# Weight loads as tasks of the planner, and tasks that look for a free buffer before they take one, in a one-core conformer and S5 decoder layer

## The chip, the core and the metric

The kernel runs on one core of a Trainium2 chip. The metric is the device time of one execution in microseconds (us). Three runs of the kernel before took 1961.82 us in the median (1961.4 to 1967.51).

## What is computed

One decoder layer is applied to 2048 new tokens of one sequence and to 8 single tokens of other sequences (`sample`). The width is 1024. The core of the reference:

```
h = rmsnorm(x, g_pre);  proj = h @ w_in            # 1024 -> 6144 columns
c_a, c_b, c_z, s_x, s_z, g_c, g_s = split(proj)    # 1024 x3, 512 x2, 1024 x2
u   = c_a * sigmoid(c_b)
v   = silu(layernorm(depthwise_conv31(u))) * silu(c_z);   y_c = v @ w_pc
ys  = gelu(ssm(s_x))                               # 32 groups x 64 complex states, scan over time
ys  = ys * sigmoid(ys @ w_glu + b_glu) * silu(s_z);       y_s = ys @ w_ps
m   = sigmoid(g_c) * y_c + sigmoid(g_s) * y_s
x   = x + rmsnorm(m @ w_out, g_post)
e   = rmsnorm(p @ w_ple, g_ple)
y   = x + e * sigmoid(x @ w_pg + b_pg)
```

The last rows of `u` and the last SSM state are outputs too.

## The kernel before

Channels lie on the partitions and tokens on the free dimension. The tokens are worked in two halves: h = 0 has 1032 of them (1024 and the 8 samples), in blocks of 344 columns, and h = 1 has 1024, in blocks of 512. In the two matrices at a half's end (`w_out`, `w_pg`) the first half goes by two parts of 516 columns, each in blocks of 258.

**Matmuls.** Weights and activations are split into a high and a low part, and each 128x128 tile of weights takes three matmuls: high by high, high by low, low by high (L289 to L291; the helper `stage_pair`, L307 to L309, does two chunks together). The low part of an activation is made on DVE or POOL after the high part was cast on ACT: `hh`/`hl` for the half's input, `mh`/`ml` for later ones.

**Weights.** The weights come in 194 chunks of 512 KB in a fixed list, `order`. A chunk is loaded into one of two `raw` buffers (`w_dma`), then split by `w_split`: ACT casts two `whi` tiles (L252), POOL subtracts to make two `wlo` tiles. There are four `whi` and four `wlo` tiles, so two chunks. `take`, which every matrix stage calls first, calls `w_ahead(i, ahead)`, and that splits the chunks up to i + ahead and issues loads up to i + 2 + ahead.

**The DMA queue.** Nearly every transfer is issued by SP, in program order (`dma`, L153). If a transfer waits for its buffer or for its data, the ones behind it wait too.

**Background work.** Everything besides the weight matmuls is written as generators, called tasks: the setting up of the SSM tables (`ssm_setup`), the SSM of a quarter of the groups (`ssm_batch`), the convolution, norms, gates. `Background` holds the tasks with priorities and keeps a clock for each engine from costs per instruction. A task yields an engine and the time from which it can go on. After each matmul block `pump` runs those tasks whose time has come, lowest priority number first. The order in which the tasks emit their instructions becomes the program order of every engine, and no engine leaves its program order. A change of one task's planned time can therefore move instructions on all engines.

**Buffers.** Large tiles come from 38 units (`Units`); `alloc` takes the next free one in the plan, and `room(k)` makes a task yield in steps of 0.5 us of planned time until k units are free.

**The places that matter below:**
- The SSM set-up. DVE builds a table of powers by seven doubling steps for each of two sets (`ph`), 12 small instructions a step, tiles of 8 up to 512 columns. Then it makes `gt`, which PE transposes (L610), and ACT copies the result into `we` (L613). The first convolution tile begins meanwhile: DVE sets its buffer's edge and starts `acc`, and ACT and POOL do a part of the 31 taps (`cq` on ACT, L882; the add to `ca` on POOL).
- The `re` sums: DVE or POOL adds squares (`rt`, squared on ACT) for a norm that is needed much later.
- The end of a half. DVE rescales the eight `o` tiles by the norm `oacc`, adds the residual `xr`, and ACT and DVE split them into `mh` and `ml` for `w_pg`. For each of eight channel tiles and each part, `y_task` loads `e`, makes `sgp` and stores it to `out_yT`.
- The boundary between halves. `next_h_task` loads eight tiles `xn`, scales them on DVE and splits them into `hh` and `hl`, which the first matmuls of h = 1 read.

## Time and profile before

| what | value |
|---|---|
| median of three runs | 1961.82 us (1961.4 to 1967.51) |
| the profiled execution | 1960.78 us |
| its span | 1959.0 us |
| mean granted clock of TensorE | 0.991 |
| PE busy | 1915.9 us (98%) |
| DVE busy | 1438.4 us (73%) |
| ACT busy | 769.3 us (39%) |
| POOL busy | 784.2 us (40%) |
| DMA queue 1, share of 16 engines | 37.0% |

The span is the time from the first to the last instruction of the profiled execution; the device time has 1.78 us around it. PE is the bound: it is idle for some 43 us in the span, part of it at the start and at the end. The rest of the idle time lies in a dozen places, the longest 14.06 us.

### The profile page before, as it was taken

The numbers are of one execution on the slowest core, as the hardware profiler recorded it, in microseconds if no ns is written. First come the engines' busy times: TensorE is split into PE (matmuls) and PEld (weight loads), VectorE is DVE, ScalarE is ACT, GpSimd is POOL, SyncE is SP. The second block draws the span as 40 slices with busy tenths as digits, with TensorE's granted clock in tenths as the row PEclk, the third lists the DMA queues.
The fourth block names the chain that finished last, engine by engine and source line by source line (L and its number), as shares of the span: only waits on it lengthen the run. The fifth ranks groups of instructions, "written<-read, shape, count | busy, mean of one in ns | idle before, by whom it ended". The sixth has DMA issues, their size and how long they took to land.

```text
span 1959.0 us, 27432 instructions
## 1 busy us (share of the span) xinstructions
PE 1915.9 (98%) x10772; PEld 1723.5 (88%) x10772; DVE 1438.4 (73%) x1703; ACT 769.3 (39%) x1301; POOL 784.2 (40%) x573
## 2 busy tenths in 40 slices
PE   8897999999999999999999999999999999999998
PEld 7897999999999999999997888888788888888876
DVE  6889997899899876446674579888499843341786
ACT  7424211228311364255533223455731353223542
POOL 1437523315422233234452222786743223224554
PEclk9898999999999999999999999999999999999999
DMA  8461334542122215334564563222112311432455
GB/s 316 152 209 56 106 133 142 181 141 71 57 89 80 99 43 194 120 95 144 193 207 162 183 204 119 65 65 97 66 43 76 99 65 44 161 108 86 140 193 172
DMA packets 103290, 243.63 MB, mean 124 GB/s; under 512 B 11752, under 2 KB 41576, under 8 KB 103144
## 3 DMA queue, kind: packets, MB, share of 16 engines
q1 hardware_dynamic: 102840, 241.68, 37.0%
q8 instruction: 84, 1.38, 0.3%
q14 instruction: 46, 0.38, 0.1%
q10 hardware_dynamic: 320, 0.20, 0.0%
HBM read 188.17 MB, written 54.62 MB: 124 GB/s over the span
## 4 chain that ended last, share of the span: by engine, by line
PE 84%; DVE 4%; issue 3%; POOL 2%; ACT 2%; DMA 1%; SPq 0%; ACTq 0%; POOLq 0%; DVEq 0%
PE bank L289 27%; PE bank L291 26%; PE bank L290 26%; PE bank L775 2%; POOL ca L332 1%; PE bank L778 1%; PE bank L720 1%; DVE sgp L332 1%; POOL wlo L332 1%; DVE o L183 1%; DMA raw<-in_w 1%; DVE spar L183 0%; DVE o L332 0%; PE bank L620 0%; DMA xn<-in_xT 0%
## 5 line engine op out<-in xcount | busy, mean ns | idle before, releaser
L332 POOL TENSOR_TENSOR wlo<-raw,whi 128x512 fp32r<-128x512 f32 x386 | 565.7, 1484 | 1072.2 <-ACT whi L252 1056.8
L289 PE MATMUL bank<-hh,whi 128*128 128x344 f32 (+1 forms) x1888 | 666.1, 353 | 0.9 <-ACT whi L252 0.9
L290 PE MATMUL bank<-hl,whi 128*128 128x344 f32 (+1 forms) x1888 | 661.4, 350 | 5.3 <-DVE hl L332 5.3
L291 PE MATMUL bank<-hh,wlo 128*128 128x344 f32 (+1 forms) x1888 | 659.8, 349 | 1.5 <-POOL wlo L332 1.5
L183 DVE SCALAR_TENSOR_TENSOR acc<-u,prm,acc 128x1024 f32<-128x1024 f32 x412 | 530.5, 1288 | 11.2
L289 PEld LDWEIGHTS bank<-hh,whi 128*128 128x128 f32 x1888 | 356.6, 189 | 37.5 <-ACT whi L252 1.5
L290 PEld LDWEIGHTS bank<-hl,whi 128*128 128x128 f32 x1888 | 357.1, 189 | 36.8 <-DVE hl L332 5.6
L291 PEld LDWEIGHTS bank<-hh,wlo 128*128 128x128 f32 x1888 | 357.4, 189 | 34.7 <-POOL wlo L332 2.5
L252 ACT CAST whi<-raw 128x512 fp32r<-128x512 f32 x388 | 223.9, 619 | 144.0 <-PE bank L290 68.7
L289 PE MATMUL bank<-mh,whi 128*128 128x258 f32 (+1 forms) x768 | 247.0, 322 | 2.2 <-ACT mh L339 1.7
L291 PE MATMUL bank<-mh,wlo 128*128 128x258 f32 (+1 forms) x768 | 246.6, 321 | 1.7 <-POOL wlo L332 1.6
L290 PE MATMUL bank<-ml,whi 128*128 128x258 f32 (+1 forms) x768 | 246.5, 321 | 0.4 <-DVE ml L332 0.3
L291 PEld LDWEIGHTS bank<-mh,wlo 128*128 128x128 f32 x768 | 145.6, 190 | 14.3 <-POOL wlo L332 3.0
L289 PEld LDWEIGHTS bank<-mh,whi 128*128 128x128 f32 x768 | 145.4, 189 | 14.2 <-ACT mh L339 1.9
L290 PEld LDWEIGHTS bank<-ml,whi 128*128 128x128 f32 x768 | 145.5, 189 | 12.5 <-DVE ml L332 1.0
L332 POOL TENSOR_TENSOR ca<-ca,cq 128x512 f32<-128x512 f32 x104 | 132.3, 1300 | 38.9 <-ACT cq L882 35.6
L290 PE MATMUL bank<-vl,whi 128*128 128x344 f32 (+1 forms) x320 | 111.9, 350 | 0.7 <-DVE vl L332 0.7
L289 PE MATMUL bank<-vh,whi 128*128 128x344 f32 (+1 forms) x320 | 112.0, 350 | 0.0
L291 PE MATMUL bank<-vh,wlo 128*128 128x344 f32 (+1 forms) x320 | 111.9, 350 | 0.0
L882 ACT ACTIVATE cq<-u,prm 128x512 f32<-128x512 f32 x104 | 73.4, 722 | 55.1 <-POOL ca L332 46.0
L332 DVE TENSOR_TENSOR oacc<-oacc,sq 128x258 f32<-128x258 f32 (+1 forms) x42 | 29.7, 721 | 70.2 <-ACT sq L1389 69.9
L177 DVE TENSOR_TENSOR gcl<-bank,gcl 128x344 f32<-128x344 f32 (+1 forms) x40 | 23.5, 587 | 65.4 <-PE bank L291 65.3
(213 smaller groups left out, 2452.0 us busy)
## 6 DMA issues: line engine op xcount, KB each, us to landing
raw<-in_w SPq DMA_DIRECT2D x194, 512.0 KB
cq<-cq SPq DMA_DIRECT2D x12, 512.0 KB
e<-e SPq DMA_DIRECT2D x8, 516.0 KB
rt<-e SPq DMA_DIRECT2D x8, 516.0 KB
gc<-gc SPq DMA_DIRECT2D x8, 516.0 KB
m<-gs SPq DMA_DIRECT2D x8, 516.0 KB
gcl<-gc SPq DMA_DIRECT2D x8, 516.0 KB
m2l<-m SPq DMA_DIRECT2D x8, 516.0 KB
```

The costliest lines, as they stand in the source:

```text
L177: V.tensor_tensor(out=out, in0=a, in1=b, op=op)
L183: V.scalar_tensor_tensor(out=out, in0=a, scalar=s, in1=b, op0=op0, op1=op1)
L252: S.copy(out=hi, in_=t[:, c])
L289: T.matmul(o, hi[:, w], rh[:, c0:c0 + n], start=kt == 0, stop=False)
L290: T.matmul(o, hi[:, w], rl[:, c0:c0 + n], start=False, stop=False)
L291: T.matmul(o, lo[:, w], rh[:, c0:c0 + n], start=False, stop=kt == k - 1)
L332: (V if e == "V" else GP).tensor_tensor(out=out, in0=a, in1=b, op=op)
L720: T.matmul(pvs[rr][half_[i], jj], we[:, g * P + rr * 64:g * P + rr * 64 + 64], U[:, g, 8:8 + ne], start=True, stop=True)
L775: T.matmul(pvs[i][:, jj], TW[:, :, 2 * j + i], U[:, 2 * j + i, o0:136], start=True, stop=False)
L778: T.matmul(pvs[i][:, jj], cq[half_[i], x * 512 + j * P:x * 512 + (j + 1) * P], X[half_[i], x, j, o0:136], start=False, stop=x == 1)
L882: S.activation(out=q[:, h], in_=u[:, k + x * 512:k + x * 512 + 512], func=AF.Identity, scale=w(k))
```

## The change

`w_ahead` no longer issues the loads that are ahead. For each it adds a task, `w_load_task(i)`, with a priority below all others' numbers, so it goes first; in the plan it waits until 0.8 us after the `raw` buffer of that chunk is free, and then issues the load. A split whose chunk has not been loaded still issues the load itself (`w_load`). Besides this, seven places of four tasks now yield until one or two units are free before they take one. Which instructions there are hardly changes: the matmuls are the same, POOL and ACT have a few more convolution taps and DVE fewer.

```diff
-        wstate = {"dma": 0, "split": 0, "use": 0, "raw": [0.0, 0.0]}
+        wstate = {"dma": 0, "asked": 0, "split": 0, "use": 0, "raw": [0.0, 0.0]}
...
+        def w_load(i):
+
+            while wstate["dma"] <= i:
+                w_dma(wstate["dma"])
+                wstate["dma"] += 1
+
+        def w_load_task(i):
+
+            yield None, wstate["raw"][i % 2] + 0.8
+            w_load(i)
+
         def w_ahead(i, ahead=1):
 
             while wstate["split"] < min(i + 1 + ahead, len(order)):
-                while wstate["dma"] <= wstate["split"]:
-                    w_dma(wstate["dma"])
-                    wstate["dma"] += 1
+                w_load(wstate["split"])
                 w_split(wstate["split"], "G" if wstate["split"] else "V")
                 wstate["split"] += 1
-            while wstate["dma"] < min(i + 3 + ahead, len(order)):
-                w_dma(wstate["dma"])
-                wstate["dma"] += 1
+            while wstate["asked"] < min(i + 3 + ahead, len(order)):
+                if wstate["asked"] >= wstate["dma"]:
+                    bg.add(w_load_task(wstate["asked"]), -5 + 1e-4 * wstate["asked"])
+                wstate["asked"] += 1
...
                 r1 = use("V", 6 * cV(512), r1)
+                yield from room(1)
                 we = alloc(name="we")
...
                 free(gt)
+                yield from room(1)
                 yield "V", r3
                 kdu = alloc(name="kd")
...
                 free(kdu, we)
+                yield from room(1)
                 cq = alloc(name="cq")
...
             r = max(r1, rp)
+            yield from room(2)
             tmp, tm2 = alloc(name="stmp"), alloc(name="stmq")
...
             def gelu_task(b):
+                yield from room(1)
                 yield "S", ready[b]
+                yield from room(1)
                 zs[b] = alloc(name="z")
...
             def ysn_task(b):
+                yield from room(2)
                 yield "S", ready[b]
+                yield from room(2)
                 ysn[b] = hilo("yn")
```

What moves is seen at three places.

**DVE in the SSM set-up**, where the first convolution tile begins (`u`, `usm`, `tails`, `acc`) among the steps of the doubling (`ph`, `spar`). Before:

```order
L177 TENSOR_TENSOR ph_1651<-ph_1649 128x8x2
L177 TENSOR_TENSOR ph_1651<-ph_1650 128x8x2
L177 TENSOR_TENSOR ph_1649<-ph_1651 128x8x2
L177 TENSOR_TENSOR ph_1651<-ph_1649,ph_1650 128x8x2
L177 TENSOR_TENSOR ph_1651<-ph_1650,ph_1649 128x8x2
L177 TENSOR_TENSOR ph_1650<-ph_1651 128x8x2
L828 MEMSET u_1457 128x30
L829 COPY usm<-u_1457 128x8
L832 COPY tails<-u_1457 128x30
L180 TENSOR_SCALAR acc<-u_1457,prm 128x1024
```

And now:

```order
L177 TENSOR_TENSOR ph_1305<-ph_1304,ph_1303 128x512
L177 TENSOR_TENSOR ph_1304<-ph_1305 128x8x64
L842 MEMSET u_1429 128x30
L843 COPY usm<-u_1429 128x8
L846 COPY tails<-u_1429 128x30
L180 TENSOR_SCALAR acc<-u_1429,prm 128x1024
L585 COPY ph_1721<-spar_725 128x8
L585 COPY ph_1722<-spar_725 128x8
L177 TENSOR_TENSOR spar_725<-ph_1721 128x8
```

The convolution's start stood behind the first two steps of the second set; it now stands ahead of the whole second set. On PE the first transposes of `gt` stand 48 matmuls later than before.

**SP at the boundary of the halves**: the loads of `xn`, of weights (`raw`) and the stores of the first half's outputs. Before, with the fourth `xn` first:

```order
L153 DMA xn_10370<-in_xT 128x1024
L153 DMA raw<-in_w 128x1024
L153 DMA e_10414<-e_89 128x516
L153 DMA out_yT<-sgp_10233 128x516
L153 DMA raw<-in_w 128x1024
L153 DMA xn_10460<-in_xT 128x1024
L153 DMA xn_10467<-in_xT 128x1024
L153 DMA xn_10474<-in_xT 128x1024
L153 DMA xn_10481<-in_xT 128x1024
L153 DMA out_yT<-sgp_10302 128x516
L153 DMA out_yT<-sgp_10378 128x516
L153 DMA raw<-in_w 128x1024 x2
```

And now, with the fifth `xn` first:

```order
L153 DMA xn_10316<-in_xT 128x1024
L153 DMA e_10355<-e_89 128x516
L153 DMA out_yT<-sgp_10245 128x516
L153 DMA raw<-in_w 128x1024
L153 DMA e_10424<-e_89 128x516
L153 DMA xn_10457<-in_xT 128x1024
L153 DMA out_yT<-sgp_10321 128x516
L153 DMA raw<-in_w 128x1024
L153 DMA xn_10477<-in_xT 128x1024
L153 DMA raw<-in_w 128x1024
L153 DMA xn_10486<-in_xT 128x1024
L153 DMA out_yT<-sgp_10390 128x516
```

The last four `xn` stood together behind the load of chunk 103; now the fifth stands ahead of the load of chunk 101, the sixth and seventh ahead of those of 102 and 103, and only the eighth behind 103.

**DVE and SP at the end of the first half**, in its second part. DVE before, up to the last `ml`, with the multiplications of `e` and `sgp` between:

```order
L183 SCALAR_TENSOR_TENSOR o_8114<-o_8114,prm,oacc_8116 128x516
L183 SCALAR_TENSOR_TENSOR o_8115<-o_8115,prm,oacc_8116 128x516
L183 SCALAR_TENSOR_TENSOR e_9606<-e_9606,prm,re_8669 128x516
L332 TENSOR_TENSOR sgp_9570<-sgp_9570,e_9606 128x516
L332 TENSOR_TENSOR sgp_9570<-sgp_9570,o_8112 128x516
L183 SCALAR_TENSOR_TENSOR e_9677<-e_9677,prm,re_8669 128x516
L332 TENSOR_TENSOR sgp_9641<-sgp_9641,e_9677 128x516
L332 TENSOR_TENSOR sgp_9641<-sgp_9641,o_8113 128x516
L332 TENSOR_TENSOR o_8114<-o_8114,xr_9713 128x516
L332 TENSOR_TENSOR o_8115<-o_8115,xr_9717 128x516
L332 TENSOR_TENSOR ml_7908<-o_8114,mh_7907 128x516
L332 TENSOR_TENSOR ml_8007<-o_8115,mh_8006 128x516
```

And now:

```order
L183 SCALAR_TENSOR_TENSOR o_8141<-o_8141,prm,oacc_8143 128x516
L183 SCALAR_TENSOR_TENSOR o_8142<-o_8142,prm,oacc_8143 128x516
L342 TENSOR_TENSOR sgp_9419<-sgp_9419,e_9453 128x516
L342 TENSOR_TENSOR sgp_9419<-sgp_9419,o_8137 128x516
L342 TENSOR_TENSOR o_8141<-o_8141,xr_9616 128x516
L342 TENSOR_TENSOR o_8142<-o_8142,xr_9646 128x516
L183 SCALAR_TENSOR_TENSOR e_9526<-e_9526,prm,re_8672 128x516
L342 TENSOR_TENSOR ml_7935<-o_8141,mh_7934 128x516
L342 TENSOR_TENSOR ml_8034<-o_8142,mh_8033 128x516
```

The last `ml` was the 45th instruction from the norm's first on; it is now the 33rd. On SP the load of chunk 93 stood behind one store of that stretch; it now stands behind three:

```order
L153 DMA raw<-in_w 128x1024
L153 DMA e_9765<-e_89 128x516
L153 DMA out_yT<-sgp_9492 128x516
L153 DMA out_yT<-sgp_9574 128x516
L153 DMA out_yT<-sgp_9654 128x516
L153 DMA raw<-in_w 128x1024
```

The last of these stores waits for the 41st DVE instruction from the norm's first on. The same two shifts are found at the end of the second half.

## Rows read from the trace of the kernel before

**Rows 1.** The page: busy times, and the chain that ended last by engine.

```profile
PE 1915.9 (98%) x10772; PEld 1723.5 (88%) x10772; DVE 1438.4 (73%) x1703; ACT 769.3 (39%) x1301; POOL 784.2 (40%) x573
...
PE 84%; DVE 4%; issue 3%; POOL 2%; ACT 2%; DMA 1%; SPq 0%; ACTq 0%; POOLq 0%; DVEq 0%
```

**Rows 2.** Waits of SP's queue: us in total, times, longest.

```profile
SPq L153 <- POOL wlo L332: 1218.7, 173, 20.0
...
SPq L153 <- DVE sgp L332: 61.7, 19, 21.5
```

**Rows 3.** Timeline of DVE: start, us, operation, idle before and its releaser.

```profile
104.14 1.23 DVE L332 TENSOR_TENSOR re<-re,rt 128x1032 f32<-128x1032 f32 x1 [4.85 <-ACT rt L985]
```

**Rows 4.** Timeline of ACT, about 107 us.

```profile
106.85 1.16 ACT L252 CAST whi<-raw 128x512 fp32r<-128x512 f32 x2
```

**Rows 5.** Stretches: length, PE, PEld, DVE, ACT, POOL busy, clock, DMA.

```profile
145.10:147.00 1.90, 1.90 (x14) 1.90 (x14) 1.69 (x15) 0.00 (x0) 0.00 (x0) 1.00 0.86 303
152.70:164.00 11.30, 11.30 (x73) 11.30 (x72) 11.09 (x14) 5.61 (x10) 11.03 (x9) 1.00 0.23 66
...
173.60:186.80 13.20, 8.57 (x55) 8.29 (x53) 12.99 (x13) 4.65 (x7) 13.00 (x10) 0.91 0.14 40
187.90:192.90 5.00, 0.00 (x0) 0.00 (x0) 4.79 (x14) 0.00 (x0) 0.00 (x0) 0.50 0.14 52
```

**Rows 6.** Timelines of DVE, PE and POOL around the first transposes.

```profile
195.44 0.69 DVE L177 TENSOR_TENSOR gt<-gw 128x512 f32<-128x512 f32 x1
...
196.23 0.66 PE L610 MATMUL bank<-ident,gt 128*128 128x128 f32 x2 [14.06 <-issue]
...
198.64 1.28 POOL L332 TENSOR_TENSOR ca<-ca,cq 128x512 f32<-128x512 f32 x1 [12.04 <-ACT cq L882]
```

**Rows 7.** Timelines of PE, ACT and SP's queue at the first half's end.

```profile
989.09 0.39 PE L289 MATMUL bank<-mh,whi 128*128 128x258 f32 x1 [1.67 <-ACT mh L339]
989.82 0.58 PE L290 MATMUL bank<-ml,whi 128*128 128x258 f32 x1 [0.35 <-DVE ml L332]
...
988.41 0.62 ACT L339 CAST mh<-o 128x516 fp32r<-128x516 f32 x1 [7.96 <-DVE o L332]
...
980.92 0.33 SPq L153 DMA_DIRECT2D raw<-in_w  x1
```

**Rows 8.** Stretches, as in group 5: the first half's end and the boundary.

```profile
952.00:990.30 38.30, 36.19 (x294) 35.37 (x293) 37.87 (x41) 15.01 (x31) 18.46 (x12) 0.99 0.63 197
...
980.00:1000.00 20.00, 17.98 (x133) 17.37 (x133) 17.59 (x19) 5.82 (x12) 10.20 (x7) 0.91 0.55 180
...
1040.00:1060.00 20.00, 18.08 (x71) 13.96 (x69) 9.56 (x9) 4.73 (x6) 0.00 (x0) 0.91 0.42 144
```

**Rows 9.** Timelines of SP's queue, DVE and PE at the boundary of the halves.

```profile
1039.84 2.55 SPq L153 DMA_DIRECT2D xn<-in_xT  x4
...
1046.49 1.28 DVE L183 SCALAR_TENSOR_TENSOR xn<-xn,prm,rb 128x1024 f32<-128x1024 f32 x1 [5.99 <-DMA xn<-in_xT]
...
1048.91 0.50 PE L307 MATMUL bank<-hh,whi 128*128 128x512 f32 x1 [1.16 <-ACT hh L339]
1050.17 0.49 PE L308 MATMUL bank<-hl,whi 128*128 128x512 f32 x1 [0.76 <-DVE hl L332]
...
1060.77 0.50 PE L308 MATMUL bank<-hl,whi 128*128 128x512 f32 x1 [0.43 <-DVE hl L332]
```

**Rows 10.** Second half's end: PE and ACT timelines, and a piece of the chain.

```profile
1901.07 0.50 PE L289 MATMUL bank<-mh,whi 128*128 128x512 f32 x1 [0.51 <-ACT whi L252]
1902.92 0.50 PE L291 MATMUL bank<-mh,wlo 128*128 128x512 f32 x1 [1.13 <-POOL wlo L332]
1915.13 0.51 PE L291 MATMUL bank<-mh,wlo 128*128 128x512 f32 x1 [0.51 <-POOL wlo L332]
...
1911.32 1.22 ACT L339 CAST mh<-o 128x512 fp32r<-128x512 f32 x2 [8.17 <-DVE o L332]
...
1904.59 3.57 DMA raw<-in_w
```

## The prediction

> **What bounds the kernel now.** I read the page first. PE is busy 1915.9 of 1959.0 us and carries 84% of the chain that ended last [rows 1]. The matmuls stay the same, so the change can only move what PE waits for. That is 43 us in all, and a gain can't be larger than that and the clock lost behind it.
>
> The next view is the waits of SP's queue [rows 2]. 173 waits for `wlo` add up to 1218.7 us: most of the time the queue's head is a weight load whose `raw` buffer is still in use. This is what the change is about. But a waiting head costs time only where something behind it is late for PE, and PE's own waits, read from the timelines, tell where that is:
>
> - the SSM set-up, 14.06 us before the first transposes of `gt` [rows 6]
> - the first half's end, 1.67 and 0.35 us for `mh` and `ml` [rows 7]
> - the boundary, 1.16, 0.76 and 0.43 us for `hh` and `hl`, which come from `xn` [rows 9]
> - the second half's end, 0.51, 1.13 and 0.51 us for split weights [rows 10]
>
> The remaining waits lie where the order does not change, or are shorter. I go through these four places with the new order.
>
> **The set-up.** Before: DVE stands 4.85 us until an `rt` square lets it go on at 104.14 [rows 3]. The stretches then show the doubling steps at two prices [rows 5]. The step of 16 columns took 1.90 us with POOL idle, that of 64 columns 11.30 with POOL busy, that of 256 columns 13.20 with POOL busy, and that of 512 columns only 5.00 when POOL had stopped. So beside POOL's adds a small DVE instruction takes 0.8 us in place of 0.1. POOL stopped because ACT, in program order, stands at its `we` copy and sends no `cq`: POOL was idle for 12.04 us up to 198.64 [rows 6], so the adds end at 186.6.
>
> Now three things differ.
>
> 1. The `rt` square stands on ACT behind a `whi` cast that ends at 108.0 [rows 4]. With about 1.1 for the square DVE goes on at 109.1, 5.0 later.
> 2. The convolution starts ahead of the second set, not behind two of its steps. Before, those steps ended at 147.0. Now it starts at 147.0 + 5.0 - 3.8 = 148.2 and ends near 149.5. The step of 8 columns follows to 151.4. POOL's adds begin near 152.4 as before (ACT is held by PE there).
> 3. ACT has 21 `cq` ahead of its `we` copy instead of 19, so the adds end at 186.6 + 2 x 1.28 = 189.2.
>
> The steps of 16, 32 and 64 columns fall under the adds: 3 x 11.3, and with three evictions of `u` 1.5, to 186.8. The step of 128 is half free, 4.0 (between 1.90 and 11.30), to 190.8. The step of 256 is free, 3.4 (between 1.90 and 5.00), to 194.2, and that of 512 ends at 199.2. Small ones and two more evictions take 2.8, half a `gt` 2.0: 204.0. Before it was 195.44 + 0.69 = 196.1 [rows 6], so `gt` comes 7.9 later. PE meanwhile does the 48 matmuls that now stand ahead of the transposes, 73 in 11.3 us [rows 5], so 7.4. Term: **+0.5**. PE's wait stays near 14 us and moves. Bounds: -6, if the steps of 16 and 32 columns under the adds cost nearer 8 than 11.3; above, the second rival.
>
> A rule of the Trainium skill speaks against this place. The page "SBUF — State Buffer", section "SBUF: two separate sides", says that DVE instructions with two SBUF inputs and GpSimd instructions that read SBUF take turns on a shared port pair, each holding it for its whole length. The prices of [rows 5] agree. By that rule alone the 24 instructions moved under the adds would come on top in full, which is the second rival's time; the rows add that the adds run out.
>
> **The first half's end.** 41 DVE instructions took 37.87 us there [rows 8], 0.92 each, and ACT stood 7.96 us for the last `o` [rows 7]. The last `ml` moves from the 45th to the 33rd instruction after the norm, so it is done 11 us sooner. That removes 1.67 + 0.35 and the clock behind it. The granted clock of 980 to 1000 is 0.91 [rows 8], a stretch at 1.2 GHz worth 0.09 x 20 = 1.8. Together -3.8. What is late next is the load of chunk 93. It was issued at 980.92 [rows 7], and now stands behind a store that needs the 41st DVE instruction. The 45th ended at 990.3, so the 41st at 986.6. With 3.57 to land [rows 10] the chunk is there at 990.3. Its split, before, came just behind the `mh` casts at about 990.3 and would be wanted 3.8 sooner: late by up to 3.8, by 0 if the chunk in PE's hands covers it. I take 1.5. Term: **-2.3**.
>
> **The boundary.** SP issued the last four `xn` together at 1039.84, and DVE stood 5.99 us for the first of them until 1046.49 [rows 9]. Now the fifth, sixth and seventh stand ahead of the loads of chunks 101 to 103, so they are issued from about 1028 on. Only the eighth is issued near 1040, and PE wants it last: it came to the fifth at 1048.91 - 1.16 = 1047.75 [rows 9], and three tiles follow. DVE had room, 9.56 of 20 us busy from 1040 [rows 8]. The three waits go, 2.35, and the clock behind them, again 0.91 over 20 us [rows 8], 1.8. Term: **-4.15**. Bounds: 0, if the new order of stores holds the queue, and -4.15.
>
> **The second half's end.** The same two shifts. ACT was held 8.17 us for `o` until 1911.32 [rows 10], and casts of weights stood behind it; with `o` earlier the waits of 0.51 + 1.13 + 0.51 = 2.15 go. The load of 1904.59 [rows 10] now stands behind the fifth store, whose DVE instruction is the 39th after the norm. The 45th was near 1913, so the 39th 6 x 0.92 earlier, 1907.5, and the load is 2.9 later; with 3.57 it lands at 1911, about when ACT gets to it. I take 0.5 (0 to 3). Term: **-1.65**.
>
> **Everything else.** The plan changes on all engines, but between these places PE's operands are early, and 17 more adds on POOL and 13 us less on DVE lie beside PE work. A new plan can still put small waits elsewhere. Those shown are 0.35 to 1.67 each [rows 7, 9, 10]. I take two or so: **+2**, between 0 and 5. The other `room` waits move tasks within stretches where PE does not wait for them; were the cover gone, they would show as such waits.
>
> **Sum.** 0.5 - 2.3 - 4.15 - 1.65 + 2 = -5.6 on the profiled execution's 1960.78 us: 1955.2. The median of the runs is 1.04 above that execution, so the forecast is **1956.2 us**. A measurement of this kernel can tell about 0.3% from no change, 5.9 us, so this lies at the edge of what it can tell. Its own range, from the bounds of the terms, is 1951 to 1962.
>
> **The rivals.**
>
> - **The set-up gets cheaper too.** If the narrow steps under the adds cost 8 us in place of 11.3 and the adds end at 187, `gt` comes 6 us sooner: 1950. For it: few elements in those steps. Against it: the price looks to be one per instruction, not per element [rows 5].
> - **The adds don't run out.** If ACT keeps sending `cq` while DVE works through its steps, two steps are added at 11.3 - 1.9 = 9.4 each and none is given back. `gt` is then later by 5.0 + 18.8 - 1.2 (an `re` add that went to POOL) = 22.6, less PE's 7.4: 15.2, in place of 0.5. Time: 1956.2 + 14.7 = 1971, slower. It decides by the number of adds before the transposes: 21 by my count, some 33 for this. Against it: POOL's 12.04 idle [rows 6].
> - **Stores hold the weights.** At both ends of a half stores now stand ahead of loads; SP already waited up to 21.5 us for an `sgp` [rows 2]. If DVE needs 1.1 us or more per instruction, several chunks come late, the gains of 2.3 and 1.65 are lost and some 6 is added: 1966.
> - **It does not matter.** The loads wait for the same buffers, and a wait that goes is replaced by the next: 1961.
>
> **Chances.** Forecast 0.52, half of it under 1955.9; cheaper set-up 0.15; adds go on 0.12; stores hold the weights 0.11; no matter 0.10. Faster: 0.26 + 0.15 = 0.41. Same: 0.26 + 0.10 = 0.36. Slower: 0.12 + 0.11 = 0.23. The range reaches from 1948, under the first rival, to 1970, which leaves out most of the second.
>
> **What would show it.** Right: PE's wait at L610 still 10 to 18 us, ended at about 204; no waits for `hh` or `hl` at the boundary, and `xn` issued one by one; no wait of over 1 us for `mh` at the first half's end. Wrong: a wait at L610 of over 22 us or under 8; PE waiting for `whi` or `wlo` behind a load that SP held for `sgp`; new waits of more than 5 us in all elsewhere.

## The result, and the profile after

The changed kernel took **1978.65 us** in the median of four runs (1976.58 to 1980.45), the kernel before 1961.61 beside it (1957.31 to 1967.51). The ratio is 1.0084, with a 95% interval of 1.0056 to 1.0113. So it is slower, by 17 us, where 1956.2 was forecast; the time lies outside the range (1948 to 1970). The profiled execution took 1980.45 us with a span of 1978.7, 19.7 more than before; it is the slowest of the four, 1.8 above their median. One execution of a later run, that with tasks for chunks 100 to 103, had a granted clock of 0.655 and took 2652.25 us, and it is left out of that run's median.

The page of the changed kernel, as [rows 1] before:

```profile
PE 1925.5 (97%) x10772; PEld 1732.0 (88%) x10772; DVE 1440.0 (73%) x1692; ACT 783.9 (40%) x1318; POOL 795.9 (40%) x590
...
PE 41%; issue 3%; POOL 2%; DVE 1%; ACT 1%; DMA 1%; SPq 0%; POOLq 0%; ACTq 0%
```

PE is busy 9.6 us longer with the same 10772 matmuls, so some of them ran at a lower clock; the rest of the 19.7 is idle time. PE's waits in the changed kernel (us in total, times, longest):

```profile
PE bank L621 <- DVE gt L177: 9.8, 1, 9.8
PE bank L301 <- POOL wlo L342: 9.0, 10, 1.9
...
PE bank L299 <- DVE u L177: 4.2, 1, 4.2
PE bank L299 <- ACT vh L349: 2.5, 2, 1.8
PE bank L789 <- DMA tw<-tt: 1.6, 1, 1.6
PE bank L300 <- DVE vl L342: 1.5, 2, 0.8
```

The wait of 14.06 for `gt` [rows 6] has become two, 9.8 and 4.2. New are those for `vh` and `tw`; there are more for `wlo`, and two for `vl` where there was one of 0.72. Here is where they lie, in PE's timeline (start, us, operation, idle before and its releaser):

```profile
183.58 0.66 PE L299 MATMUL bank<-hh,whi 128*128 128x344 f32 x1 [4.20 <-DVE u L177]
207.26 1.12 PE L621 MATMUL bank<-ident,gt 128*128 128x128 f32 x4 [9.79 <-DVE gt L177]
...
278.30 1.20 PE L789 MATMUL bank<-U,tw 128*128 128x136 f32 x4 [1.57 <-DMA tw<-tt]
...
498.08 0.43 PE L301 MATMUL bank<-hh,wlo 128*128 128x344 f32 x1 [1.91 <-POOL wlo L342]
...
768.09 0.42 PE L300 MATMUL bank<-vl,whi 128*128 128x344 f32 x1 [0.84 <-DVE vl L342]
770.51 0.66 PE L299 MATMUL bank<-vh,whi 128*128 128x344 f32 x1 [1.84 <-ACT vh L349]
...
999.82 0.39 PE L301 MATMUL bank<-mh,wlo 128*128 128x258 f32 x1 [1.28 <-POOL wlo L342]
1014.54 0.47 PE L299 MATMUL bank<-mh,whi 128*128 128x258 f32 x1 [2.92 <-ACT whi L252]
1016.37 0.58 PE L301 MATMUL bank<-mh,wlo 128*128 128x258 f32 x1 [1.13 <-POOL wlo L342]
...
1061.57 0.50 PE L319 MATMUL bank<-hh,wlo 128*128 128x512 f32 x1 [0.65 <-POOL wlo L342]
...
1920.19 0.50 PE L299 MATMUL bank<-mh,whi 128*128 128x512 f32 x1 [0.58 <-ACT whi L252]
1922.04 0.50 PE L301 MATMUL bank<-mh,wlo 128*128 128x512 f32 x1 [1.11 <-POOL wlo L342]
```

Behind most of them PE ran at half speed for a while; behind those at 999.82 and 1061.57 the granted clock stayed at 1.00. Stretches of the changed kernel (length, busy PE, PEld, DVE, ACT, POOL, granted clock, DMA share, GB/s):

```profile
278.00:290.00 12.00, 10.95 (x52) 10.18 (x52) 5.89 (x6) 1.91 (x4) 1.28 (x1) 0.72 0.21 73
...
498.00:503.00 5.00, 4.92 (x21) 4.92 (x22) 4.86 (x5) 1.02 (x2) 5.00 (x5) 0.66 0.35 105
...
766.00:776.00 10.00, 6.04 (x20) 5.00 (x20) 6.70 (x7) 4.58 (x6) 3.03 (x2) 0.66 0.29 101
```

In 498 to 503 PE waits 0.08 us and yet loses 5.00 x 0.34 = 1.7: the second price of a wait of 1.91.

**Where the time went.** Both traces hold the same number of matmuls, so the end of the n-th matmul can be compared between two runs, at places where their orders agree. The difference to the kernel before, in us, for the changed kernel and for runs that are explained below (their first column of numbers, at matmul 762, shows how far runs differ before the orders do):

| up to matmul (us before) | 762 (150) | 1100 (219) | 1700 (307) | 3036 (510) | 4494 (740) | 4741 (780) | 6185 (970) | 8399 (1400) | 10754 (1950) |
|---|---|---|---|---|---|---|---|---|---|
| changed | 1.0 | 3.5 | 7.6 | 12.0 | 11.7 | 17.8 | 19.3 | 18.2 | 19.7 |
| tasks for chunks 2 to 25 | 0.5 | 3.3 | 5.6 | 6.9 | 7.9 | 14.8 | 14.3 | 12.5 | 12.8 |
| for 10 to 25 | 0.5 | 3.2 | 3.3 | 3.0 | 2.8 | 6.4 | 6.4 | 6.1 | 5.6 |
| for 26 to 83 | 0.0 | -0.2 | -0.2 | -0.3 | -0.3 | -0.2 | 0.6 | -0.5 | -0.6 |
| for 84 and on | 0.1 | 0.2 | 0.2 | 0.3 | 0.3 | 0.3 | 0.3 | -1.7 | 0.0 |
| for 100 to 103 | 2.2 | 1.2 | 1.2 | 1.2 | 1.2 | 1.2 | 1.2 | -3.5 | -3.4 |
| changed, norm earlier | 0.1 | 2.6 | 4.9 | 7.7 | 7.5 | 7.3 | 8.0 | 7.5 | 9.3 |

So in this execution of the changed kernel the set-up cost 2.5 (to matmul 1100), the stretch with the wait near 278 4.1, the next, with the wait near 498, 4.4, the `vh` stage 6.0, and one near 945 most of 1.5 more. The half's end and the boundary together gave back 1.1, and the second half's end cost 1.5.

### The profile page after: what moved, and what is told of

Its sections match the earlier page's. It is cut to its first block, busy times and chain, and to the rows that moved or that the text cites. A ratio compares the mean times of both kernels' runs of the same rounds, so it can differ in the third digit from the quotient of the medians.

```text
span 1978.7 us, 27479 instructions
## 1 busy us (share of the span) xinstructions
PE 1925.5 (97%) x10772; PEld 1732.0 (88%) x10772; DVE 1440.0 (73%) x1692; ACT 783.9 (40%) x1318; POOL 795.9 (40%) x590
## 5 line engine op out<-in xcount | busy, mean ns | idle before, releaser
L342 POOL TENSOR_TENSOR wlo<-raw,whi 128x512 fp32r<-128x512 f32 x386 | 556.7, 1461 | 1067.8 <-ACT whi L252 1050.2
L183 DVE SCALAR_TENSOR_TENSOR acc<-u,prm,acc 128x1024 f32<-128x1024 f32 x406 | 522.8, 1288 | 11.1
L342 POOL TENSOR_TENSOR ca<-ca,cq 128x512 f32<-128x512 f32 x116 | 147.8, 1305 | 39.6 <-ACT cq L896 39.4
L300 PEld LDWEIGHTS bank<-ml,whi 128*128 128x128 f32 x768 | 146.2, 190 | 11.7
L896 ACT ACTIVATE cq<-u,prm 128x512 f32<-128x512 f32 x116 | 81.6, 721 | 56.4 <-POOL ca L342 54.6
L177 DVE TENSOR_TENSOR gcl<-bank,gcl 128x344 f32<-128x344 f32 (+1 forms) x40 | 23.5, 587 | 67.6 <-PE bank L301 67.6
```

The source lines that it names most:

```text
L177: V.tensor_tensor(out=out, in0=a, in1=b, op=op)
L183: V.scalar_tensor_tensor(out=out, in0=a, scalar=s, in1=b, op0=op0, op1=op1)
L300: T.matmul(o, hi[:, w], rl[:, c0:c0 + n], start=False, stop=False)
L342: (V if e == "V" else GP).tensor_tensor(out=out, in0=a, in1=b, op=op)
L896: S.activation(out=q[:, h], in_=u[:, k + x * 512:k + x * 512 + 512], func=AF.Identity, scale=w(k))
```

## The experiments

All times are medians, with the ratio to the kernel before and its 95% interval from runs on the same chip.

### Which loads make it

The branch that adds the task gets a condition; chunks outside it are loaded at once, three ahead, as before. The five runs differ in the condition alone. (The seven waits for a free buffer stand in all of them. In the run with tasks for chunks 100 to 103 PE and POOL do all they do in the order of before, and ACT and SP do up to the boundary, so these waits by themselves move nothing there.)

```diff
                 if wstate["asked"] >= wstate["dma"]:
-                    bg.add(w_load_task(wstate["asked"]), -5 + 1e-4 * wstate["asked"])
+                    if wstate["asked"] < 26:
+                        bg.add(w_load_task(wstate["asked"]), -5 + 1e-4 * wstate["asked"])
+                    else:
+                        w_load(wstate["asked"])
```

> The changed kernel, but only the loads of chunks 2 to 25 are tasks (the SSM set-up and what runs beside it); the later chunks are loaded three ahead. Theory F: the waits of the set-up stay, 9.8 for gt and about 4 for u, and the load of tw behind the scan's units near 278 with its half-speed stretch too; the rest of the program falls back to what it was, so 1961.6 + 0.6 + 3 + 5.7 = 1969 to 1973. Theory S: nothing of it remains and the time is that of before, 1960 to 1963.

> Only the loads of chunks 10 to 25 are tasks. Up to about 120 us every engine has the order of the kernel before, so DVE's stand of 12 us at 110 is not there (4.85 as before), but the adds of the convolution and the doubling steps change their order as in the changed kernel. Theory D (DVE's stands in the set-up make the loss): 1962 to 1968. Theory P (the steps that come under POOL's adds make it, gt about 10 us later whatever stood before): 1971 to 1975, as with the loads of chunks 2 to 25.

> Only the loads of chunks 26 to 83 are tasks. The set-up is as before. Theory D: with DVE's work on time through the set-up, the middle of the first half keeps its cover and the time is that of before, 1960 to 1963. Theory P (late loads make small waits of their own wherever they stand, as the 1.9 at 498 and 1.3 at 945): 1964 to 1968.

> The changed kernel, but only the loads of chunks 84 and on are tasks; the chunks before are loaded three ahead, as before. Up to about 930 us every engine has the order of the kernel before. Theory F (what was lost lies in the set-up and in new small waits up to 930 us, with the half-speed stretches behind them): those go, the boundary's gain of about 6 stays and the loss at the halves' ends of about 8 too, so 1961 to 1965. Theory S (stores hold the weights, and that is most of the loss): 1970 or more. Theory L (loads held back cost wherever they are, through later chunks everywhere): the second half alone keeps about half of the 17 us, so 1968 to 1972.

> Only the loads of chunks 100 to 103, the four at the boundary of the halves, are tasks; SP's queue alone changes much (three stores of sums and of the output move ahead of loads), ACT and DVE have one cast and one subtraction in another place. If the boundary's gain in the prediction (4.15: three waits of 2.35 and the clock behind them) is as it was put there, and needs nothing of the rest of the change: 1960.5 - 4 = 1955 to 1958, faster than both kernels. If it is swallowed by the waits of the second half, or lay in other loads: 1959.5 to 1962.

| tasks for chunks | us | ratio |
|---|---|---|
| all (the change) | 1978.65 | 1.0084 [1.0056, 1.0113] |
| 2 to 25 | 1974.28 | 1.0068 [1.0055, 1.0080] |
| 10 to 25 | 1964.66 | 1.0023 [1.0014, 1.0032] |
| 26 to 83 | 1961.99 | 1.0004 [0.9995, 1.0013] |
| 84 and on | 1961.73 | 1.0006 [0.9997, 1.0015] |
| 100 to 103 | 1959.3 | 0.9990 [0.9981, 0.9999] |

The 24 loads of the set-up make 13 of the 17 us (1974.28 against 1960.48 beside it; theory F had 1973 at most). But most of that does not arise in the set-up: by the table of places 2.8 of it do, 2.3 near 278, and 6.9 at `vh`, long after the last of these loads. The time with 10 to 25 alone lies where theory D had it, though the next sections show that DVE's stands are not the reason. The loads of chunks 26 to 83 alone cost nothing that can be told from none. Those from 84 on give back at the half's end and at the end what they gain at the boundary. The four of the boundary alone gain 3.5 in the trace from matmul 6646 (1030 us) to 8399; in the medians it is 1.7, and the interval reaches from 0.2 to 3.7. In that trace two waits are left at the boundary, both for weights and none for `xn`, and the granted clock behind them is 1.00 where it was 0.91 before [rows 8]:

```profile
1038.34 0.50 PE L320 MATMUL bank<-hh,whi 128*128 128x512 f32 x1 [1.43 <-ACT whi L252]
1039.84 0.51 PE L322 MATMUL bank<-hh,wlo 128*128 128x512 f32 x1 [0.78 <-POOL wlo L345]
...
1050.00:1070.00 20.00, 20.00 (x88) 16.23 (x87) 8.92 (x9) 7.12 (x11) 6.08 (x4) 1.00 0.35 109
```

### Loads ahead of the stores

One line is added to `y_task`, to the changed kernel and to the one with tasks from 84 on.

```diff
                 yield None, r
+                w_load(wstate["asked"] - 1)
                 dma(out=O[f"yT{h}"][c * P:(c + 1) * P, cc], in_=sg[:, cc])
```

> The changed kernel, with one line added: before each store of the output, the weight loads that have been asked for and still stand as tasks go into SP's queue first. Theory S (stores hold the weights): in the changed kernel, PE's waits at both halves' ends, 1.28 + 1.28 + 2.92 + 1.13 us from 945 to 1017 and 0.60 + 0.58 + 1.11 from 1914 to 1922, come from loads behind stores, and 10.3 us at half speed lie behind them. They go, and the time falls from 1978.7 by 8 to 12, to 1967 to 1971. Theory F (the first half's earlier part, up to 930 us, holds the loss): these waits come from elsewhere or are replaced, and the time stays at 1976 to 1980.

> Both of these: only chunks 84 and on as tasks, and the loads that have been asked for ahead of each store of the output. If both theories hold their parts, all that is left is the gain at the boundary (4.25 us of waits and about 1.7 of half speed) and what of the waits at the halves' ends goes: 1961.6 - 6 and up to 4 less, so 1952 to 1957, faster than both kernels. If the waits at the halves' ends do not come from the order of loads and stores: 1961 to 1965, as without this line. If the gain at the boundary comes only with the stores ahead of the loads: 1961.

The first took 1974.78 (1.0071 [1.0058, 1.0083]), the second 1962.68 (1.0012 [1.0003, 1.0021]). The first lies between the two theories, and the second is no better than the same kernel without the line. Theory S holds for two of the seven waits that it names. In the changed kernel SP's queue stood at three stores ahead of a load, and ACT then stood 7.48 us for that chunk. SP and ACT of the changed kernel:

```profile
1000.35 7.56 SPq L153 DMA_DIRECT2D out_yT<-sgp  x3
1008.00 1.14 SPq L153 DMA_DIRECT2D raw<-in_w  x1
...
1013.88 1.14 ACT L252 CAST whi<-raw 128x512 fp32r<-128x512 f32 x2 [7.48 <-DMA raw<-in_w]
```

With the line the waits of 2.92 and 1.13 behind it are gone, and from matmul 6185 to 6646, the half's end, 0.2 is lost in place of 4.3 (with tasks from 84 on 0.6 in place of 3.0). The other five stay: the two of 1.28 are 0.95 and 1.27, and those at the second half's end are 0.64, 0.54 and 1.12, the last of them this one:

```profile
1918.15 0.50 PE L301 MATMUL bank<-mh,wlo 128*128 128x512 f32 x1 [1.12 <-POOL wlo L342]
```

At the boundary PE has new waits for weights, because ACT stands for an `xn` of DVE ahead of the cast that PE needs. PE and ACT of the run with the line:

```profile
1054.03 0.50 PE L317 MATMUL bank<-hh,whi 128*128 128x512 f32 x1 [1.09 <-ACT whi L252]
1056.15 0.80 PE L319 MATMUL bank<-hh,wlo 128*128 128x512 f32 x1 [1.39 <-POOL wlo L342]
...
1051.68 1.05 ACT L349 CAST hh<-xn 128x1024 fp32r<-128x1024 f32 x1 [5.44 <-DVE xn L183]
```

From matmul 6646 to 8399 the changed kernel gains 5.3 us on the kernel before and with the line 1.5; with tasks from 84 on it is 5.0 without the line and 0.2 with it. Behind matmul 10510, at the second half's end, it is better again, by 1.8 and 1.6. In the changed kernel that is clock and not waits: 0.88 over 10 us behind 1915, 1.00 at the same place with the line. So the line takes one loss away and makes another.

### The set-up

First theory D, that DVE's stands cause the later waits. DVE stood 27.4 us for squares `rt` from 95 to 745 us, where it had been 4.85 [rows 3].

```diff
-                        r = ew(e, acc[:, 0:n], acc[:, 0:n], t[:, 0:n], ALU.add, n, r)
+                        r = ew(e, acc[:, 0:n], acc[:, 0:n], (t if e == "G" else acc)[:, 0:n], ALU.add, n, r)
```

> The changed kernel with the order of every engine as it is; only those adds of the squared sums (re) that stand on DVE add the sum to itself, not the square that ACT makes, so DVE does not stand behind ACT for them. It leaves these squares out of the sums. In the changed kernel DVE stood 27.4 us for them between 95 and 745 us (11.9 at 110 and 11.3 at 485 the longest), in the kernel before 4.8. Theory D (DVE is nearly full from 100 to 745, and what it stands there comes out as PE's waits for u, gt, and vh and vl near 770): u's wait of 4.2 goes and gt comes earlier, the conv's norm is done some 20 us earlier, the waits of 3.95 near 770 go with their stretch at half speed (6 us in all), and the set-up gives 2 to 6 back: 1978.7 less 8 to 12, so 1966 to 1971. Theory P (PE's waits come from the new places of loads and steps, and DVE's idle time costs nothing): 1976 to 1980.

It took 1977.03 (1.0082 [1.0068, 1.0096]): the theory fell. DVE goes on, but only as far as the next instruction in its order that needs PE, and stands there. DVE of this run:

```profile
131.20 0.52 DVE L177 TENSOR_TENSOR u<-bank,sg 128x344 f32<-128x344 f32 x1 [10.25 <-PE bank L301]
```

DVE's idle time from 100 to 745 us, added up over its timeline, is 85.1 here, 86.1 in the changed kernel and 67.6 before.

Then the steps beside POOL's adds, with POOL's adds for the first tile narrowed, in both kernels:

```diff
+        side_h = [0]
...
+            side_h[0] = h
...
-                    left["r"] = free_at[x] = ew("G", a2[:, h], a2[:, h], q[:, h], ALU.add, 512, r)
+                    z = slice(x * 512, x * 512 + 16) if c == 0 and side_h[0] == 0 else h
+                    left["r"] = free_at[x] = ew("G", a2[:, z], a2[:, z], q[:, z], ALU.add, 512, r)
```

> The changed kernel with the order of every engine as it is; POOL's adds for the convolution of the first column tile in the first half are 16 columns wide in place of 512 (most of that part of the sum is left out). Theory C (the doubling steps that come under these adds take 13.7, 7.8 and 10.3 us in place of about 2, and that makes gt late and DVE late for the rest of the first half): the waits for u (4.2) and gt (9.8) go, and with DVE early those near 770 (3.95) too, with their half speed: 1978.7 - 14 - 3 - 6 = 1956, between 1950 and 1962. Theory E (gt and DVE are late because of what stands ahead of the steps: evictions of u, squares, PE): the waits at 184 and 207 stay within 4 us of what they were in sum, and the time is 1973 or more.

> The same in the kernel before, with its order as it is. Theory C: the wait of 14.06 for gt goes, and the 17 us at half speed behind it: 1961 - 14 - 5 to 8, so 1938 to 1943. The changed kernel with narrow adds would then stand 8 to 16 above this one (the waits for tw and wlo at 278 and 498 and the loads behind stores are left). If it stands as far above as without (17 to 18), the set-up is no part of the loss. Theory E: 1955 or more.

Both leave out most of what these adds would sum. They took 1958.9 (0.9990 [0.9981, 0.9999]) and 1944.52 (0.9921 [0.9907, 0.9934], 1.5 above its range). Theory C holds for the set-up. The step of 8 columns in the changed kernel, and that step in the run with narrow adds:

```profile
150.20:163.90 13.70, 13.70 (x89) 13.70 (x88) 13.49 (x15) 6.66 (x10) 13.62 (x10) 1.00 0.26 86
```

```profile
150.20:156.50 6.30, 6.30 (x41) 6.30 (x41) 6.09 (x15) 3.90 (x7) 5.40 (x6) 1.00 0.52 174
```

The same 15 DVE instructions take 13.7 us beside whole adds and 6.3 beside narrow ones (POOL still has weights to split and an `re` add). From matmul 762 to 1100 both runs gain 16.6 us on the kernel before: the set-up's difference is gone. The Trainium skill's page "SBUF — State Buffer", section "SBUF: two separate sides", says that DVE instructions with two SBUF inputs and GpSimd instructions that read SBUF take turns on a shared port pair; the two rows agree. But from there to the end the changed order loses 14.9, near 278, 498, `vh` and the ends, where the order of before gains 0.5. So the set-up is some 3 of the 17 us.

The adds can also be kept off the steps with nothing left out, by a hold on the convolution:

```diff
+        set_up = []
...
                 free(*pu2)
             r1 = max(r0, r1)
+            set_up.append(r1)
...
-                while us[c] is None:
+                while us[c] is None or (h == 0 and not set_up):
```

> The kernel before, with the convolution of the first half held until the last doubling step stands on DVE, so that POOL has no adds for it beside the steps. Nothing is left out. Theory C: PE waits little or nothing for gt, so 14 us and 5 to 8 of half speed less, unless DVE, which takes more of the convolution, is then late near 756: 1938 to 1948, faster than both. Theory E: gt comes when it came and the later convolution adds waits: 1960 or more.

> The changed kernel with the same hold. Theory C: the set-up's waits of 14 go with their clock, and DVE is no longer late: 1978.7 - 14 - 3 - 3 to 6, so 1954 to 1960. With the kernel before held in the same way 10 to 17 below it, what is left of the difference comes from the rest of the first half. Theory E: 1973 or more.

They took 1965.87 (1.0029 [1.0017, 1.0040]) and 1983.47 (1.0115 [1.0101, 1.0129]): slower, though at matmul 1100 they are ahead by 16.3 and 15.7. More than that is lost at one place, the first `vh` and `vl`: 21.6 and 32.1 us (their orders differ near there; between matmuls 2560 and 5320, where they agree, it is 21.9 and 32.1). The longest wait there with the changed kernel held:

```profile
747.71 0.66 PE L299 MATMUL bank<-vh,whi 128*128 128x344 f32 x1 [10.85 <-ACT vh L349]
```

### The norm ahead of `vh`

`vh` and `vl` are parts of the convolution's result behind its norm, whose matmuls (`nh`, `nl` by `avgr`) stand in PE's order at a place that the plan chooses. First, is it DVE's work that is late? 30 of the taps made narrow, so that part of the sums is left out, order unchanged:

```diff
-                    stt(out if k == PAD else acc, u[:, k:k + HT], w(k), acc, ALU.mult, ALU.add)
+                    m = 32 if h == 0 and c >= 6 and k % 2 and k < PAD else HT
+                    stt((out if k == PAD else acc)[:, 0:m], u[:, k:k + m], w(k), acc[:, 0:m], ALU.mult, ALU.add)
```

> The changed kernel with the order of every engine as it is; 30 of DVE's convolution taps of the first half's last two column tiles are 32 columns wide in place of 1024 (some 36 us less DVE work before 690; that part of the sums is left out). Theory V (the 6.1 us lost near 767, 3.95 of waits and the half speed behind them, are there because the convolution's norm ends late on DVE): they go, 1978.7 - 6 = 1971 to 1974. Theory W (they come from the weights or from ACT there): 1977 to 1981.

It took 1979.29 (1.0087 [1.0072, 1.0101]). Theory V fell. DVE of this run only stands longer, for PE, ahead of evictions that come before its last tap, 11.24 us here and 7.48 at 658.53:

```profile
624.49 0.52 DVE L177 TENSOR_TENSOR gs<-bank,gs 128x344 f32<-128x344 f32 x1 [11.24 <-PE bank L301]
```

Then the place. The stretch from the norm's last group of matmuls to the first `vh` matmul, one row from each kernel, by how much of PE's own work (the first busy time) stands between. The counts take in the group's own six. With 270 matmuls between, before:

```profile
708.82:751.41 42.59, 42.59 (x272) 42.59 (x271) 34.10 (x25) 30.16 (x39) 13.54 (x6) 1.00 0.16 48
```

With 246, tasks for chunks 10 to 25:

```profile
715.37:754.19 38.82, 38.82 (x249) 38.82 (x247) 33.20 (x24) 28.82 (x37) 11.80 (x6) 1.00 0.14 41
```

With 222, the changed kernel:

```profile
728.15:763.15 35.00, 35.00 (x224) 35.00 (x223) 26.42 (x21) 26.71 (x35) 10.45 (x6) 1.00 0.20 63
```

With 102, the kernel before with the hold:

```profile
720.68:739.53 18.85, 16.23 (x104) 15.95 (x102) 13.14 (x10) 13.76 (x19) 4.30 (x2) 1.00 0.21 73
```

With 30, the changed kernel with the hold:

```profile
731.98:747.71 15.73, 4.88 (x32) 4.60 (x31) 10.11 (x10) 12.58 (x14) 0.00 (x0) 0.81 0.37 134
```

What each lost between matmuls 4494 and 4741, by the same comparison as in the table of places:

| matmuls between norm and `vh` | 366 | 270 | 246 | 222 | 198 | 102 | 30 |
|---|---|---|---|---|---|---|---|
| PE's work between, us | 57.8 | 42.6 | 38.8 | 35.0 | 31.2 | 16.2 | 4.9 |
| lost near `vh`, us | 0.0 | 0.0 | 3.6 | 6.0 | 6.9 | 21.6 | 32.1 |

(366 is the kernel with more sums on POOL below, 198 that with tasks for chunks 2 to 25. The run without squares, the narrow adds and the narrow taps in the changed kernel all stand at 222 and lost 6.7, 6.1 and 6.1.) The kernel before lost nothing there, and 24 matmuls less already cost 3.6. How much it had to spare is not told by PE, whose wait of 0.72 for `vl` is there with 366 matmuls between as well, 0.71. That wait ends a short chain behind PE's own last block for `cz` (the gate that the norm's result is multiplied by). DVE tells it, by how long it stood for `cz` when all that the norm feeds was done up to there: 2.41 us before, 6.65 with 366 matmuls, and not at all in the changed kernel. DVE before; DVE and PE with 366:

```profile
752.10 1.23 DVE L332 TENSOR_TENSOR cz<-cz,u 128x1032 f32<-128x1032 f32 x1 [2.41 <-ACT cz L323]
```

```profile
747.69 1.23 DVE L332 TENSOR_TENSOR cz<-cz,u 128x1032 f32<-128x1032 f32 x1 [6.65 <-ACT cz L323]
...
751.33 0.43 PE L290 MATMUL bank<-vl,whi 128*128 128x344 f32 x1 [0.71 <-DVE vl L332]
```

The test changes the plan's cost of a tap, from the last tile on, in the changed kernel:

```diff
-                    r = use("V", 1.33)
+                    r = use("V", 1.1 if h == 0 and c >= 7 else 1.33)
```

> The changed kernel, with the plan's cost of a DVE tap set to 1.1 in place of 1.33 for the last column tile of the first half, and nothing else. All orders up to there stay; the convolution's norm comes 48 matmuls earlier on PE, 270 ahead of the first use of its result, as in the kernel before. Theory N (what was lost near 767 is the place of the norm in the order, which the plan sets by the time at which it believes DVE's sums done): 5 to 6.5 us go, 1972 to 1975. Theory V (DVE really is late by as much): PE then stands at the norm's matmuls near 715 in place of 767, and the time stays at 1977 to 1981.

> The same order, with the 30 taps of the last two tiles 32 columns wide as in the run with less work on DVE. Theory N: as with the earlier norm alone, 1972 to 1975. Theory V: only here do the 6 us go; 1972 to 1975 here, 1977 to 1981 without the narrow taps.

They took 1972.18 (1.0061 [1.0047, 1.0074]) and 1973.42 (1.0062 [1.0048, 1.0076]). Theory N holds, in both. The first is 6.5 us under the changed kernel by the medians and 4.5 by the ratios, and between matmuls 4494 and 4741 it loses nothing, where the changed kernel loses 6.0. The norm is back at 270 matmuls, and of the four waits at `vh` one is left, the one that the kernel before had too. PE of the kernel with the norm earlier:

```profile
763.24 0.43 PE L300 MATMUL bank<-vl,whi 128*128 128x344 f32 x1 [0.72 <-DVE vl L342]
```

### A version faster than both

With more column tiles shared with POOL, DVE's sums end early enough, and the hold's gain can stay:

```diff
-                if units.left() >= 8:
+                if units.left() >= 6:
```

> The kernel before, with the convolution of the first half held until the last doubling step stands on DVE, and with a column tile's sum shared with POOL where 6 units are free, not 8 (408 taps on DVE in place of 452 with the hold alone). Theory V: with the hold alone DVE was late by some 27 us against PE at the convolution's norm and PE lost 22; 44 taps of 1.28 us less make it early, and the set-up's 14 us with 8.5 of half speed stay gained: 1938 to 1946, faster than both kernels. If POOL's further adds slow DVE elsewhere as they did beside the steps: 1955 to 1966.

> The changed kernel with both of these. Theory V: what the late loads cost in the set-up and at 767 hangs on DVE; with DVE early only what lies at 278, 498 and the halves' ends is left, so it comes within 4 to 9 us of the kernel before in the same form: 1943 to 1953. If the late loads cost by themselves, wherever they stand: 15 to 18 above it, 1955 to 1963.

> The kernel before with the hold and the wider sharing, and the loads of chunks 100 to 103 as tasks. If the boundary's gain (3.4 us in the trace of the run with these four alone, 1.1 in the medians) adds to it: 1 to 4 below the same without them. If not: the same within 1.5.

The kernel before with both edits took 1957.57 (0.9983 [0.9974, 0.9992]), the changed kernel with them 1971.76 (1.0052 [1.0036, 1.0067]), and the first with the four boundary loads as tasks **1956.57** (0.9974 [0.9964, 0.9984]). The last is the fastest that leaves nothing out, faster than both kernels, by 4.5 us than the kernel before in its own runs. It is 1.0 below the first, with intervals that overlap, so what the four loads add here is not clear of noise. The expectation of 1938 to 1946 for the first was missed: 16 us ahead at matmul 1100, the kernel loses 6.8 between 245 and 417 us, with a new wait of 3.6 near 249, and 3.2 more near 432.

The second pair tells something else. There PE waits for no `gt` in the set-up before 200 us (in the changed kernel there is one wait of 1.41 at 221.6) and the norm costs nothing in either kernel (it stands 366 matmuls ahead in the kernel before, 270 in the changed one), and yet the late loads cost 14.2 us, near the 17 of the original and not the 4 to 9 that theory V gave. They lie at other places; two in PE's timeline of the changed kernel in this form:

```profile
236.23 1.18 PE L736 MATMUL bank<-U,swe 128*64 128x136 f32 x8 [4.28 <-DVE u L177]
...
504.51 0.42 PE L300 MATMUL bank<-yl,whi 128*128 128x344 f32 x1 [3.09 <-POOL yl L342]
```

So each cause that was taken away in the original is shown for the original alone. Why a plan with late loads places things worse again when the places change was not found.

## Why the prediction was wrong

**The set-up: +0.5 forecast, +2.5 measured, and so near by luck.** DVE goes on after the square of `rt` at 110.0 (109.1 forecast), the convolution starts at 148.8 (148.2), 21 adds stand ahead of the transposes, and POOL then idles for 12.12 us (12.04 before, [rows 6]). But the steps between were read wrongly. The step of 8 columns was put ahead of POOL's work, at 1.9; POOL had two splits and an `re` add from 150.1 on, and it took 13.7 (the row above). The steps of 16 and 32 took 7.8 and 10.3 where 11.3 each was put. That of 64 was put under the adds, at 11.3; POOL had run out early, stood for a cast of ACT, and the step took 2.1. So 11.8 too little and 13.7 too much nearly cancel. And "the step of 256 is free, 3.4" failed, because POOL came back. POOL in the changed kernel, and the steps of 64 and of 256 columns:

```profile
187.84 1.31 POOL L342 TENSOR_TENSOR wlo<-raw,whi 128x512 fp32r<-128x512 f32 x1 [5.02 <-ACT whi L252]
...
194.85 2.73 POOL L342 TENSOR_TENSOR ca<-ca,cq 128x512 f32<-128x512 f32 x2 [0.55 <-ACT cq L896]
209.70 2.52 POOL L342 TENSOR_TENSOR ca<-ca,cq 128x512 f32<-128x512 f32 x2 [12.12 <-ACT cq L896]
```

```profile
183.40:185.50 2.10, 1.92 (x7) 1.92 (x8) 1.90 (x13) 0.00 (x0) 0.00 (x0) 0.50 0.00 0
...
191.60:199.00 7.40, 5.87 (x38) 5.58 (x36) 7.20 (x13) 2.14 (x4) 5.43 (x5) 1.00 0.00 0
```

That step took 7.4, so `gt` came at 207.2 and not at 204.0. The second rival (33 adds, 1971) did not come: there were 21.

**The first half's end: -2.3 forecast, +4.3 measured** (matmuls 6185 to 6646, 970 to 1030 us; 3.0 with tasks from 84 on alone, where nothing before differs). The waits for `mh` and `ml` went as forecast. The term for the load behind the stores, "I take 1.5", was the one mis-sized. Chunk 93 was to be issued at 986.6 and to be there at 990.3. It was issued at 1008.00, which is 988.7 once the 19.3 lost by then are taken off, behind three stores that took 7.56 us, and ACT began on it 5.88 later, not 3.57. PE waited 2.92 + 1.13 us for it, and 1.28 for a split ahead of it. With the 3.8 that did go, the term is 8.1 in place of 1.5. This is the third rival, "stores hold the weights", and the runs with the loads first show it, with 0.2 and 0.6 lost here. SP's waits for `sgp` rose from 61.7 in 19 [rows 2] to 138.3 in 31:

```profile
SPq L153 <- POOL wlo L342: 1065.7, 150, 20.0
SPq L153 <- DVE sgp L342: 138.3, 31, 14.3
```

**The second half's end: -1.65 forecast, +1.5 measured.** Here it is not the stores. The step that failed is that with `o` earlier the waits for split weights go: ACT still stood 4.95 us for `o`, until 1917.83, and the casts of weights still stood behind it. PE waited 0.60 + 0.58 + 1.11, 2.29 us where it had been 2.15, and as long with the loads first. The rest is the clock of that execution, 0.88 where the run with the loads first had 1.00.

**The boundary: -4.15 forecast, -5.3 measured.** Right in the changed kernel's trace: of the waits of 1.16, 0.76 and 0.43 for `xn` [rows 9] none is left, there is one of 0.65 for `wlo`, and from matmul 6646 to 8399 the gain is 5.3. In the trace of the four loads alone it is 3.5. The medians show 1.7 for it, with an interval up to 3.7, so its size in an average run is told less well than its mechanism.

**Everything else: +2 (0 to 5) forecast, 16 measured** (4.1 near 278, 4.4 from there to 510 us, 6.0 at `vh`, 1.5 near 945). This is the step that made the prediction wrong: "between these places PE's operands are early". How early was not read from the profile, and the new order was not held against it. At `vh` they were early by 2.41 us of DVE's time, and the new order takes 48 matmuls, 7.6 us of PE's work, away. The runs with the norm earlier show it: these 48 are worth 6.0. For `tw` the trace shows the chain: its buffer is the one that a `stmp` has just left, SP stands 16.0 us for DVE's last use of it and issues the load 14.9 us later than before, and PE is at the same place only 6 later. SP's queue in the changed kernel, and in the kernel before:

```profile
274.87 0.32 SPq L153 DMA_DIRECT2D tw<-tt  x1
```

```profile
259.94 0.32 SPq L153 DMA_DIRECT2D tw<-tt  x1
```

The cause of the wait near 498, where `wlo` stands on POOL behind other work, is read from the trace and was not tried alone; nor was another buffer for `tw`. Their sizes are those of one execution: six other traces with the same order of matmuls up to there lost 2.3 to 3.7 near 278, and in the stretch with 498 four of them 2.8 to 2.9, one 2.0 and one 4.4.

**The chances.** 0.23 stood on slower, on rivals that give 1966 and 1971. The third happened at one of its two ends and explains 6.6 of the 25 us between the 1955.2 forecast for the profiled execution and its 1980.45. No rival said that a norm is placed 48 matmuls later, though the order of the changed kernel shows it. The range of 1951 to 1962 is also narrower than the bounds of its terms: all low give 1946, all high, without the second rival, 1968.

## What to carry to other kernels

When a plan is changed, list for every result that PE consumes how many matmuls stand between the last one that feeds it and the first that needs it, in both orders, and compare what is taken away with the time for which the chain's own engine stood before the last step. Here that was 2.41 us of DVE against 7.6 us of matmuls. PE's own wait does not tell it: 0.72 us with 270 matmuls between, 0.71 with 366. Loads and stores in one queue can be an exchange: here the loads put first gained 4.1 us at the half's end, and the boundary gave 3.9 less.

## What was not expected of the hardware

- What a short wait costs in clock is not the same each time, in one and the same order. Behind one wait of 1.6 to 1.7 us near 278 the runs with the loads ahead of stores, the narrow taps and the norm earlier lost 2.3 to 2.4 between matmuls 1100 and 1700, the changed kernel 4.1 and the run without squares 3.6. In the changed kernel that is 1.57 and 0.75 us of waits and a granted clock of 0.72 over 12 us. Behind the wait of 1.91 near 498 the granted clock was 0.66 over 5 us in the changed kernel, and 1.00 behind the same wait of 1.90 with the norm earlier:

```profile
495.30:500.30 5.00, 4.96 (x31) 4.96 (x32) 4.86 (x5) 1.45 (x3) 5.00 (x4) 1.00 0.31 105
```

- DVE instructions of 8 columns, most of them with two SBUF inputs, took 0.9 us each beside POOL's splits and adds of 512 columns (13.49 busy in 15), and 0.41 beside adds of 16 columns and some splits.
